# The input norm's vectors come as single rows and are spread by TensorE, the small loads go to SyncE's queue, and the first projection's copies stand in another order

## The chip, the cores and the metric

The kernel runs on one NeuronCore of a Trainium2 chip. The metric is the device time of one execution in microseconds (us); lower is better. A profile of one execution stands beside the timed runs, and each number in this part comes from it or from the times.

## What the kernel computes

A trunk of two layers over 512 tokens of width 1024, in float32. First comes a layer norm of the input with the vectors `ln_in_g` and `ln_in_b`. Each layer then projects the tokens to 2212 columns, runs three kinds of attention on them (latent, differential with a learned lambda, and forgetting), projects back and normalises, and sends the tokens through 16 experts of which each token uses two. Cut to what matters here:

```
h = layer_norm(x, ln_in_g, ln_in_b)
for l in range(DEPTH):
    mix = mixer_sublayer(h, ..., w_in[l], ...)      # starts with proj = h @ w_in
    h = layer_norm(ALPHA * h + mix, ln1_g[l], ln1_b[l])
    h = layer_norm(ALPHA * h + grouped_moe(h, router_w, router_bias, ...), ln2_g[l], ln2_b[l])
```

## The kernel before

The 512 tokens lie in four tiles `h[:, t]` of 128 partitions by 1024. Weights come in pieces of 128x1024 (512 KB), issued by `pump` (L324) on SyncE's queue. A piece is made into two rounded parts: `prep_hi` copies it on ScalarE (L369), `prep_lo` subtracts that copy from the piece on VectorE (L376). The tokens are split likewise in `make_hT`: TensorE transposes a tile into PSUM (L741), ScalarE copies the rounded part (L743), VectorE makes the rest (L744). A product is then three matmuls, `mm3`: L400 (high by high), L401 (low tokens by high weights), L402 (high tokens by low weights).

The beginning of the program, which this change touches:

- `setup` sends dummy matmuls (`busy`, L553, one column of weights by 384 columns) and issues the first loads in the order of the string `PRO`: x tile 0, the norm's two vectors, a table, two pieces of w_in, x tile 1, two pieces, x tiles 2 and 3. `load_ln` fetches each vector as a broadcast to 128 partitions, 512 KB.
- `ln` normalises one tile: the sum (ScalarE, L699), the mean (VectorE, L703), (x - mean) * g (VectorE, L721), the sum of squares (ScalarE, L706), the power -0.5 (GpSimd, L708), and times the rstd plus b (VectorE, L725).
- `token_major` with column group c0 is the first projection: for each tile the transposes, then 24 matmuls over the four pieces, then `ev_c0` (L823 to L830, a copy and a small rotary). Group c1 follows with its own four pieces, then the attention units, filled up with the other projections.
- `rotary8` and `consts` make small tables; `consts` also issues the small loads (router weights and bias, norm gains, lambda vectors) on ScalarE's queue and computes the lambdas.
- `score_consts` (at step 40 of the attention) makes `rg`, router weights times `ln1_g`, from the columns `lncol` (L1186, L1190).

The order of the instructions on each engine is set when the program is built, by a scheduler that works with estimated times; an engine takes its instructions in this order, and a wait holds all that stand behind it. Loads on SyncE's and ScalarE's queues share eight completion semaphores (named DMAHW0 to DMAHW7 in the program), so an issue also waits until the load that had its semaphore before has landed.

Of the kernel before, what the change touches and what calls it, by code (L numbers as in the profile page):

```python
# [11 lines left out]
F32 = mybir.dt.float32  # L12
# [4 lines left out]
AF = mybir.ActivationFunctionType  # L17
OP = mybir.AluOpType
# [5 lines left out]
S = 512  # L24
NT = 4
DEPTH = 2
NE = 16
# [28 lines left out]
WARM = 40  # L56
WARM2 = 6
# [203 lines left out]
class Kern:  # L261
# [238 lines left out]
    def setup(self):  # L500
# [30 lines left out]
        self.busy(WARM)  # L531
# [70 lines left out]
    def consts(self):  # L602
# [18 lines left out]
        nc.scalar.dma_start(self.rw, I["router_w"].rearrange("(h p k) e -> p h k e", h=2, k=4))  # L621
        self.rb = c.tile([128, NE], F32, name="rb")
        nc.scalar.dma_start(self.rb, self.bcast(I["router_bias"], NE))
        v.tensor_scalar(self.rb, self.rb, 0.5, None, op0=OP.add)
# [6 lines left out]
        with nc.allow_non_contiguous_dma(reason="small vectors"):  # L631
            for l in range(DEPTH):
                nc.scalar.dma_start(self.gq[:, l], I["mla_q_norm_g"][l].rearrange("(k p) -> p k", p=128))
                nc.scalar.dma_start(self.gkv[:, l], I["mla_kv_norm_g"][l].rearrange("(k p) -> p k", p=128))
                for s in range(2):
                    nc.scalar.dma_start(self.gs[64 * s:64 * s + 64, l:l + 1],
                                        I["diff_subln_g"][l].rearrange("(p o) -> p o", o=1))
                for j, n in enumerate(("diff_lam_q1", "diff_lam_k1", "diff_lam_q2", "diff_lam_k2")):
                    nc.scalar.dma_start(self.lamv[:, l, j], self.bcast(I[n][l], 32))
                nc.scalar.dma_start(self.fb[:, l:l + 1], I["fox_f_bias"][l].rearrange("(p o) -> p o", o=1))  # L640
# [15 lines left out]
        for x in hs + [self.hc]:  # L656
            x.free()

        self.nlam = c.tile([128, DEPTH], F32, name="nlam")
# [6 lines left out]
        hl.free()  # L666
# [25 lines left out]
    def ln_stats(self, z, sums=None, then=None, eps=LN_EPS):  # L692

        nc, v = self.nc, self.nc.vector
        st = self.sm.tile([128, 6], F32, name="bst", bufs=4)
        junk = self.lnbuf[2].f
        if sums is None:
            sums = [st[:, 0:1]]
            nc.scalar.activation(junk, z, AF.Copy, accum_out=sums[0])  # L699
        if len(sums) == 2:  # L700
            v.tensor_add(st[:, 0:1], sums[0], sums[1])
            sums = [st[:, 0:1]]
        v.tensor_scalar(st[:, 1:2], sums[0], -1.0 / D, None, op0=OP.mult)  # L703
        if then:
            then(st)
        nc.scalar.activation(junk, z, AF.Square, bias=st[:, 1:2], accum_out=st[:, 2:3])  # L706
        v.tensor_scalar(st[:, 3:4], st[:, 2:3], 1.0 / D, eps, op0=OP.mult, op1=OP.add)
        self.i_pow = nc.gpsimd.tensor_tensor(st[:, 4:5], st[:, 3:4], self.mhalf, OP.pow)  # L708
        return st

    def ln(self, z, sums=None, pool=False, eps=LN_EPS, out=None):
# [12 lines left out]
        if out is None:  # L724
            v.scalar_tensor_tensor(z, w, st[:, 4:5], self.lnrow[1], op0=OP.mult, op1=OP.add)  # L725
            return
# [29 lines left out]
    def token_major(self, l, c, evac, pre=None):  # L756
        ids = [self.idx[l, c, j] for j in range(4)]
        P = [self.get(i) for i in ids]
        if pre:
            pre(0)  # L760
            pre(1)
        for t in range(NT):
            if pre:
                if l and t == 0:
                    self.busy(WARM4)
                self.make_hT(t)
                if l == 0 and t == 0:
                    self.busy(WARM2)
# [47 lines left out]
    def w_in_phase(self, l, pre):  # L816
# [5 lines left out]
        def ev_c0(t, ps):  # L822
            nc.scalar.activation(tm[t], ps, AF.Copy)  # L823
# [6 lines left out]
            v.tensor_add(x[:, :, 0:8], a, b)  # L830
# [4 lines left out]
        if l == 0:  # L835
            self.consts()
# [10 lines left out]
        def turn(g, j):  # L847
# [9 lines left out]
            for a in range(2):  # L857
                x = [self.dm[g][a].r[32 * i:32 * i + 32, 512 * j:512 * j + 512] for i in range(3)]
                y = ps[32 * a:32 * a + 32]
                nc.scalar.activation(x[0], y, AF.Copy, scale=sc)  # L860
                nc.scalar.activation(x[1 if j else 2], y, AF.Copy, scale=sc)
                if j:
                    v.tensor_sub(x[2], y, x[0].bitcast(F32))
# [15 lines left out]
        self.token_major(l, "c1", ev_c1)  # L879
        self.cap = 2  # L880
# [253 lines left out]
    def mixer(self, l, pre):  # L1134
# [5 lines left out]
        nc.gpsimd.dma_start(gc, self.I["ln1_g"][l].rearrange("(h p k) -> p h k", h=2, k=4))  # L1140
        nc.gpsimd.dma_start(bc, self.I["ln1_b"][l].rearrange("(h p k) -> p h k", h=2, k=4))
# [40 lines left out]
        def score_consts():  # L1182
# [3 lines left out]
            nc.vector.tensor_tensor(self.rg, rw, gc.rearrange("p h (k o) -> p (h k) o", o=1).to_broadcast([128, 8, NE]), OP.mult)  # L1186
# [761 lines left out]
class Unit:  # L1948
# [6 lines left out]
    def scores(self):  # L1955
# [4 lines left out]
        for m in range(self.maps):  # L1960
# [17 lines left out]
            nc.vector.tensor_tensor_reduce(out=p[:, 0:n], in0=ps[:, 0:n], in1=b, op0=OP.add, op1=OP.min,  # L1978
# [97 lines left out]
```

## Time and profile before

| | us |
|---|---|
| median of 3 runs | 1391.88 (1390.42 to 1392.33) |
| profiled execution, its own time | 1390.85 |
| its span, first to last instruction | 1389.1 |
| TensorE busy | 1303.3 (94%) |
| first matmul of the c0 projection that runs without a break behind it (L401, tile 0) | 19.21 |
| first matmul of the c1 projection | 52.03 |

The profiled execution took 1.75 us more than its span and 1.03 us less than the median. A row of a timeline gives the start, the duration, the engine, the source line and the operation, and in brackets how long the engine had been idle and what ended that; several like instructions are merged (x8). In a table of windows each engine has its busy time in the stretch, then the granted TensorE clock (1.00 is 2.4 GHz, 0.50 is 1.2 GHz), the DMA engines' busy share and what they moved in GB/s.

### The profile page before, as it was taken

The numbers are of one execution on the slowest core, as the hardware profiler recorded it, in microseconds if no ns is written. First come the engines' busy times: TensorE is split into PE (matmuls) and PEld (weight loads), VectorE is DVE, ScalarE is ACT, GpSimd is POOL, SyncE is SP. The second block draws the span as 40 slices with busy tenths as digits, with TensorE's granted clock in tenths as the row PEclk, the third lists the DMA queues.
The fourth block names the chain that finished last, engine by engine and source line by source line (L and its number), as shares of the span: only waits on it lengthen the run. The fifth ranks groups of instructions, "written<-read, shape, count | busy, mean of one in ns | idle before, by whom it ended". The sixth has DMA issues, their size and how long they took to land. (4 is left out here: it accounts for less than half of the span.)

```text
span 1389.1 us, 18769 instructions
## 1 busy us (share of the span) xinstructions
PE 1303.3 (94%) x6052; PEld 961.6 (69%) x6052; DVE 1016.0 (73%) x2289; ACT 800.3 (58%) x1429; POOL 267.3 (19%) x208
## 2 busy tenths in 40 slices
PE   8999999989999999899799989999999999979994
PEld 5786766768677776677488766676877777656773
DVE  5768977676778777677655798867768877757775
ACT  5467856551566665566336776557146666555662
POOL 1012223332111211111000222224412111102110
PEclk9999999999999999999899999999999999989998
DMA  8411312257699997999510123325679999878991
GB/s 257 127 35 31 111 62 92 85 176 259 222 306 315 338 363 252 326 398 368 191 43 16 31 80 122 99 69 166 226 249 298 307 345 362 244 279 299 384 360 61
DMA packets 114426, 290.05 MB, mean 209 GB/s; under 512 B 19751, under 2 KB 42535, under 8 KB 114321
## 3 DMA queue, kind: packets, MB, share of 16 engines
q1 hardware_dynamic: 97824, 254.31, 52.1%
q0 software_dynamic: 11136, 31.38, 9.2%
q10 hardware_dynamic: 5360, 3.10, 0.8%
q8 instruction: 50, 0.82, 0.2%
q14 instruction: 56, 0.45, 0.1%
HBM read 268.13 MB, written 27.00 MB: 212 GB/s over the span
## 5 line engine op out<-in xcount | busy, mean ns | idle before, releaser
L369 ACT ACTIVATE slot<-arena 128x1024 fp32r<-128x1024 f32 (+3 forms) x147 | 127.4, 887 | 103.1 <-PE A L402 26.6
L376 DVE TENSOR_TENSOR slot<-slot,slot 128x1024 fp32r<-128x1024 f32 x105 | 128.3, 1225 | 64.7 <-ACT slot L369 61.9
L369 ACT ACTIVATE slot<-slot 128x1024 fp32r<-128x1024 f32 x111 | 117.1, 1058 | 100.4 <-PE A L402 36.7
L402 PE MATMUL S<-slot,rounded 128*128 128x512 f32 x368 | 150.4, 409 | 0.2 <-DVE slot L1844 0.2
L402 PE MATMUL A<-slot,rounded 128*128 128x512 f32 x372 | 147.7, 397 | 0.0
L400 PE MATMUL S<-slot,rounded 128*128 128x512 f32 x316 | 138.9, 442 | 6.4 <-ACT rounded L743 4.0
L376 DVE TENSOR_TENSOR slot<-arena,slot 128x1024 fp32r<-128x1024 f32 (+2 forms) x101 | 112.8, 1120 | 42.8 <-ACT slot L369 40.5
L401 PE MATMUL S<-slot,rounded 128*128 128x512 f32 x316 | 127.7, 404 | 3.0 <-DVE rounded L744 1.7
L400 PE MATMUL A<-slot,rounded 128*128 128x512 f32 x288 | 125.4, 435 | 0.3 <-ACT rounded L743 0.3
L1571 POOL DMA_INDIRECT yD<-arena,ix x28 | 46.9, 1674 | 408.1 <-ACT rounded L1606 197.5
L401 PE MATMUL A<-slot,rounded 128*128 128x512 f32 x288 | 114.1, 396 | 0.4 <-DVE rounded L744 0.4
L1989 ACT ACTIVATE arena<-arena,ast 128x256 f32<-128x256 f32 (+3 forms) x160 | 88.9, 557 | 33.1 <-DVE ast L1978 23.9
L378 POOL TENSOR_TENSOR slot<-arena,slot 128x1024 fp32r<-128x1024 f32 (+4 forms) x46 | 70.7, 1550 | 170.2 <-ACT slot L369 148.6
L369 ACT ACTIVATE rounded<-slot 128x1024 fp32r<-128x1024 f32 x70 | 74.3, 1061 | 44.6 <-PE A L401 25.5
L400 PE MATMUL S<-rounded,slot 128*128 128x512 f32 (+1 forms) x224 | 90.5, 406 | 0.0
L401 PE MATMUL S<-rounded,slot 128*128 128x512 f32 (+1 forms) x224 | 89.8, 401 | 0.0
L402 PE MATMUL S<-rounded,slot 128*128 128x512 f32 (+1 forms) x224 | 89.2, 398 | 0.0
L402 PEld LDWEIGHTS S<-slot,rounded 128*128 128x128 f32 x368 | 70.9, 193 | 17.7 <-DVE slot L1844 2.0
L402 PEld LDWEIGHTS A<-slot,rounded 128*128 128x128 f32 x372 | 70.1, 188 | 16.3
L2020 ACT ACTIVATE slot<-T 128x128 fp32r<-128x128 f32 (+3 forms) x128 | 53.4, 431 | 48.2 <-PE T L2015 47.5
L1647 PE MATMUL A<-slot,arena 128*128 128x512 f32 x168 | 79.4, 594 | 0.5 <-ACT arena L1605 0.5
L400 PEld LDWEIGHTS S<-slot,rounded 128*128 128x128 f32 x316 | 61.1, 194 | 25.4 <-ACT rounded L743 5.0
(368 smaller groups left out, 3066.8 us busy)
## 6 DMA issues: line engine op xcount, KB each, us to landing
slot<-in_exp_w_down_dram SPq DMA_DIRECT2D x80, 512.0 KB
slot<-in_exp_w_up_dram SPq DMA_DIRECT2D x73, 512.0 KB
slot<-in_exp_w_gate_dram SPq DMA_DIRECT2D x72, 512.0 KB
arena<-in_exp_w_gate_dram SPq DMA_DIRECT2D x60, 512.0 KB
arena<-in_exp_w_up_dram SPq DMA_DIRECT2D x59, 512.0 KB
arena<-in_exp_w_down_dram SPq DMA_DIRECT2D x52, 512.0 KB
arena<-in_w_in_dram SPq DMA_DIRECT2D x14, 512.0 KB
slot<-in_w_in_dram SPq DMA_DIRECT2D x12, 512.0 KB
```

The source lines that it names most:

```text
L369: self.nc.scalar.activation(hi, r, AF.Copy)
L376: self.nc.vector.tensor_sub(lo, r, hi.bitcast(F32))
L378: self.nc.gpsimd.tensor_tensor(lo, r, hi.bitcast(F32), OP.subtract)
L400: t.matmul(ps, xh, wh, start=start, stop=False)
L401: t.matmul(ps, xl, wh, start=False, stop=False)
L402: t.matmul(ps, xh, wl, start=False, stop=stop)
L1571: self.nc.gpsimd.indirect_dma_start(out=self.yD[:, :], out_offset=bass.IndirectOffsetOnAxis(ap=ix[:, 0:1], axis=0), in_=y, in_offset=None, ...
L1647: nc.tensor.matmul(ps, xW(e)[:, kk], P.raw.f[:, 512 * k:512 * k + 512], start=kk == 0, stop=kk == 7)
L1989: nc.scalar.activation(p, p, AF.Exp, bias=self.st[:, m:m + 1], scale=-1.0, accum_out=self.st[:, 2 + m:3 + m])
L2020: nc.scalar.activation(self.part(0), self.ps, AF.Copy)
```

## The change

The two norm vectors come as one row each (4 KB) on ScalarE's queue; TensorE multiplies a 1x128 row of ones with each half row, which puts it on 128 partitions of PSUM, and VectorE (g) and ScalarE (b) copy it to SBUF. The dummy matmuls go from 40 to 8 and 14. The small loads are merged over layers and issued from SyncE's queue; the lambdas are computed after the c1 projection. `token_major` prepares the first pieces in an order written out by hand, and `issue_after` holds groups of instructions behind named ones of the same engine.

```
-WARM = 40
+WARM = (8, 14)
...
-                self.load_ln(I["ln_in_g"], I["ln_in_b"], nc.sync)
+                self.spread_ln(I["ln_in_g"], I["ln_in_b"])
...
+    def spread_ln(self, g, b):
+        nc = self.nc
+        self.lnbuf = [self.unit(self.A) for _ in range(5)]
+        self.iw = 1
+        self.lnrow = [x.f for x in self.lnbuf[0:2]]
+        one = self.cp.tile([1, 1], F32, name="one")
+        nc.vector.memset(one, 1.0)
+        rows = [x.f[0:1] for x in self.lnbuf[3:5]]
+        for row, x in zip(rows, (g, b)):
+            nc.scalar.dma_start(row, x.rearrange("(o d) -> o d", o=1))
+        self.busy(WARM[0])
+        self.lps = [self.psS.tile([128, 512], F32, name="S") for _ in range(4)]
+        for j, ps in enumerate(self.lps):
+            nc.tensor.matmul(ps, one.to_broadcast([1, 128]), rows[j // 2][:, 512 * (j % 2):512 * (j % 2) + 512], start=True, stop=True)
+        self.busy(WARM[1])
+        nc.vector.tensor_copy(self.lnrow[0][:, 0:512], self.lps[0])
...
-        nc.scalar.dma_start(self.rw, I["router_w"].rearrange("(h p k) e -> p h k e", h=2, k=4))
+        nc.sync.dma_start(self.rw, I["router_w"].rearrange("(h p k) e -> p h k e", h=2, k=4))
...
-            for l in range(DEPTH):
-                nc.scalar.dma_start(self.gq[:, l], I["mla_q_norm_g"][l].rearrange("(k p) -> p k", p=128))
...
+            nc.sync.dma_start(self.gq, I["mla_q_norm_g"].rearrange("l (k p) -> p l k", p=128))
...
+        lps = getattr(self, "lps", None)
+        if lps:
+            v.tensor_copy(self.lnrow[0][:, 512:1024], lps[1])
...
+        if lps:
+            with self.tc.issue_after(i.ins):
+                for n in range(2):
+                    self.i_b = nc.scalar.activation(self.lnrow[1][:, 512 * n:512 * n + 512], lps[2 + n], AF.Copy)
...
+        if pre and l == 0:
+            self.prep_limit = 1
+            self.prep()
+            self.prep_limit = 2
             pre(0)
-            pre(1)
+            with self.tc.issue_after(self.i_b.ins):
+                with self.tc.issue_after(self.i_ln.ins):
+                    self.prep_low(1)
+                    self.make_hT(0)
+                    self.busy(WARM2)
+                    P = [self.get(i) for i in ids[:2]]
+                    self.prep_limit = len(self.pieces)
+                    pre(1)
+                    P += [self.get(i) for i in ids[2:]]
...
-        nc.gpsimd.dma_start(gc, self.I["ln1_g"][l].rearrange("(h p k) -> p h k", h=2, k=4))
+        nc.sync.dma_start(gc, self.I["ln1_g"][l].rearrange("(h p k) -> p h k", h=2, k=4))
...
-            nc.vector.tensor_tensor(self.rg, rw, gc.rearrange("p h (k o) -> p (h k) o", o=1).to_broadcast([128, 8, NE]), OP.mult)
+            with self.tc.issue_after(self.i_red.ins):
+                nc.vector.tensor_tensor(self.rg, rw, gc.rearrange("p h (k o) -> p (h k) o", o=1).to_broadcast([128, 8, NE]), OP.mult)
```

VectorE at the start of the program, before (`bst` holds a tile's norm statistics, `arena` is the shared SBUF region that holds x times g and the weight pieces, `slot` a piece's rounded part, `T` and `S` are PSUM):

```order
L588 CAST arena<-arena 128x4
L1186 TENSOR_TENSOR rg<-rw,lncol_698 128x128
L703 TENSOR_SCALAR bst<-bst 128x1
L624 TENSOR_SCALAR rb<-rb 128x16
L721 SCALAR_TENSOR_TENSOR arena<-h,bst,arena 128x1024
L707 TENSOR_SCALAR bst<-bst 128x1
L725 SCALAR_TENSOR_TENSOR h<-arena,bst 128x1024
L376 TENSOR_TENSOR slot_162<-arena,slot_161 128x1024
L672 TENSOR_SCALAR gs<-gs 128x1
L376 TENSOR_TENSOR slot_165<-arena,slot_164 128x1024
L744 TENSOR_TENSOR rounded<-T,rounded 128x512
```

The same place after (the lines are those of the changed file: L723 is L703 of before, L749 L721, L753 L725, L772 L744, L605 L588):

```order
L585 COPY arena<-S 128x512
L726 COPY arena<-S 128x512
L723 TENSOR_SCALAR bst<-bst 128x1
L749 SCALAR_TENSOR_TENSOR arena<-h,bst,arena 128x1024
L735 TENSOR_SCALAR bst<-bst 128x1
L753 SCALAR_TENSOR_TENSOR h<-arena,bst 128x1024
L376 TENSOR_TENSOR slot_150<-arena,slot_149 128x1024
L376 TENSOR_TENSOR slot_194<-arena,slot_193 128x1024
L772 TENSOR_TENSOR rounded<-T,rounded 128x512 x2
L723 TENSOR_SCALAR bst<-bst 128x1
L605 CAST arena<-arena 128x4
L376 TENSOR_TENSOR slot_227<-arena,slot_226 128x1024
```

Ahead of tile 0's mean there now stand the two copies of g, and no longer `rg`, `rb`, `gs` or the cast of the positions.

ScalarE at the same place, before, with the loads that it issues:

```order
L699 ACTIVATE arena,bst<-h 128x1024
L634 DMA gkv<-in_mla_kv_norm_g_dram 128x2x1
L706 ACTIVATE arena,bst<-h,bst 128x1024
L636 DMA gs<-in_diff_subln_g_dram 64x1 x2
L639 DMA arena<-in_diff_lam_k_dram 128x32
L640 DMA fb<-in_fox_f_bias_dram 4x1
L633 DMA gq<-in_mla_q_norm_g_dram 128x3x1
L369 ACTIVATE slot_161<-arena 128x1024
L634 DMA gkv<-in_mla_kv_norm_g_dram 128x2x1
L636 DMA gs<-in_diff_subln_g_dram 64x1
L369 ACTIVATE slot_164<-arena 128x1024
L743 ACTIVATE rounded<-T 128x512
```

And after (L719 is L699 of before, L729 L706, L771 L743, L604 the issue of the positions):

```order
L719 ACTIVATE arena,bst<-h 128x1024
L369 ACTIVATE slot_149<-arena 128x1024
L729 ACTIVATE arena,bst<-h,bst 128x1024
L733 ACTIVATE arena<-S 128x512 x2
L369 ACTIVATE slot_193<-arena 128x1024
L719 ACTIVATE arena,bst<-h 128x1024
L604 DMA arena<-in_positions_dram 128x4x1
L771 ACTIVATE rounded<-T 128x512 x2
```

The eight small loads between tile 0's sum and the copy of its transposes are gone from ScalarE; the load of the positions moved from the program's start to here, and the copies of b came in.

VectorE ahead of tile 1's low part (the second L772 of tile 1 follows later):

```order
L700 TENSOR_SCALAR arena<-arena 128x16
L723 TENSOR_SCALAR bst<-bst 128x1
L701 TENSOR_SCALAR arena<-arena 128x16
L749 SCALAR_TENSOR_TENSOR arena<-h,bst,arena 128x1024
L702 SCALAR_TENSOR_TENSOR arena<-arena 128x16
L703 SCALAR_TENSOR_TENSOR arena<-arena 128x16
L735 TENSOR_SCALAR bst<-bst 128x1
L704 SCALAR_TENSOR_TENSOR arena<-arena 128x16
L753 SCALAR_TENSOR_TENSOR h<-arena,bst 128x1024
L705 TENSOR_SCALAR arena<-arena 128x16
L772 TENSOR_TENSOR rounded<-T,rounded 128x512
```

The whole norm of x tile 2 (L749, L753) stands ahead of the low part of tile 1 (L772); before, only its first half stood there.

## Rows read from the trace of the kernel before

**Rows 1.** The page, busy time of each engine, share of the span, instructions

```profile
PE 1303.3 (94%) x6052; PEld 961.6 (69%) x6052; DVE 1016.0 (73%) x2289; ACT 800.3 (58%) x1429; POOL 267.3 (19%) x208
```

**Rows 2.** The timeline of the first 20 us, tile 0's chain

```profile
4.84 1.06 ACT L699 ACTIVATE arena<-h 128x1024 f32<-128x1024 f32 x1 [2.12 <-DMA h<-in_x_dram]
...
5.54 0.17 DVE L588 CAST arena<-arena 128x4 f32<-128x4 int32 x1 [3.98 <-DMA arena<-in_positions_dram]
...
9.14 0.29 DVE L1186 TENSOR_TENSOR rg<-rw,lncol 128x128 f32<-128x128 f32 x1 [3.43 <-DMA rw<-in_router_w_dram]
...
9.54 1.15 ACT L706 ACTIVATE arena<-h,bst 128x1024 f32<-128x1024 f32 x1 [3.54 <-DVE bst L703]
...
11.05 0.57 POOL L708 TENSOR_TENSOR bst<-bst,mhalf 128x1 f32<-128x1 f32 x1 [8.12 <-DVE bst L707]
...
11.65 1.28 DVE L725 SCALAR_TENSOR_TENSOR h<-arena,bst 128x1024 f32<-128x1024 f32 x1 [0.69 <-POOL bst L708]
...
12.99 1.16 PE L741 MATMUL T<-cst,h 128*128 128x128 f32 x8 [1.32 <-DVE h L725]
...
16.24 1.06 ACT L369 ACTIVATE slot<-arena 128x1024 fp32r<-128x1024 f32 x1 [2.63 <-DMA gs<-in_diff_subln_g_dram]
...
17.21 0.58 ACT L743 ACTIVATE rounded<-T 128x512 fp32r<-128x512 f32 x1
...
19.21 0.79 PE L401 MATMUL S<-slot,rounded 128*128 128x512 f32 x1 [0.58 <-DVE bst L703]
```

**Rows 3.** Windows: stretch, length, busy of the engines, clock, DMA share, GB/s

```profile
5.00:6.00 1.00, 1.00 (x5) 0.42 (x4) 0.17 (x1) 0.99 (x2) 0.00 (x0) 1.00 1.01 377
...
14.00:15.00 1.00, 0.41 (x3) 0.08 (x1) 0.87 (x1) 0.00 (x0) 0.00 (x0) 1.00 0.55 70
17.00:18.00 1.00, 0.16 (x1) 0.17 (x1) 0.67 (x1) 1.00 (x3) 0.00 (x0) 0.66 1.07 406
24.00:25.00 1.00, 1.00 (x5) 0.79 (x4) 0.83 (x1) 0.25 (x2) 0.00 (x0) 0.92 0.21 61
38.00:40.00 2.00, 2.00 (x7) 1.54 (x6) 0.40 (x4) 0.00 (x0) 0.00 (x0) 0.50 1.11 277
```

**Rows 4.** The timeline of TensorE, tiles 1 to 3 and the c1 projection

```profile
28.02 0.47 PE L401 MATMUL A<-slot,rounded 128*128 128x512 f32 x1
...
37.48 0.53 PE L401 MATMUL S<-slot,rounded 128*128 128x512 f32 x1 [1.75 <-DVE rounded L744]
...
44.50 1.05 PE L741 MATMUL T<-cst,h 128*128 128x128 f32 x8
...
52.03 0.40 PE L400 MATMUL S<-slot,rounded 128*128 128x512 f32 x1
```

**Rows 5.** Waits of SyncE's queue to 60 us: total, times, longest

```profile
SPq L324 <- DMA gs<-in_diff_subln_g_dram: 5.0, 2, 4.0
```

**Rows 6.** The timeline, prices: dummy matmuls, VectorE's spacing, plain float32 matmuls

```profile
6.83 0.13 PEld L553 LDWEIGHTS <-b_zero 128*1 128x1 bf16 x1 [0.19 <-issue]
7.13 4.15 PEld L553 LDWEIGHTS <-b_zero 128*1 128x1 bf16 x26 [0.17 <-issue]
...
19.25 1.28 DVE L721 SCALAR_TENSOR_TENSOR arena<-h,bst,arena 128x1024 f32<-128x1024 f32 x1
...
20.46 1.22 DVE L376 TENSOR_TENSOR slot<-arena,slot 128x1024 fp32r<-128x1024 f32 x1
...
350.29 1.88 PE L1647 MATMUL A<-arena 128*128 128x512 f32 x4
```

**Rows 7.** Groups by line and form, VectorE: busy, mean ns, idle before

```profile
L918 DVE COPY arena<-S 128x512 f32<-128x512 f32 x7 | 4.8, 692 | 9.3 <-PE S L402 9.3
```

**Rows 8.** The timeline, later: SyncE's queue and the use of lncol

```profile
87.98 0.56 SPq L324 DMA_DIRECT2D slot<-in_w_in_dram  x1
...
238.65 0.95 PE L1190 MATMUL S<-rw,lncol 128*1 128x16 f32 x32
...
250.44 0.34 SPq L324 DMA_DIRECT2D arena<-in_exp_w_gate_dram  x1
```

More of the change, by code (lines that the diff above doesn't have):

```diff
@@ L631, in consts @@
         with nc.allow_non_contiguous_dma(reason="small vectors"):
-            for l in range(DEPTH):
-                nc.scalar.dma_start(self.gq[:, l], I["mla_q_norm_g"][l].rearrange("(k p) -> p k", p=128))
[L634 to L640, printed above, removed]
+            nc.sync.dma_start(self.gq, I["mla_q_norm_g"].rearrange("l (k p) -> p l k", p=128))
+            nc.sync.dma_start(self.gkv, I["mla_kv_norm_g"].rearrange("l (k p) -> p l k", p=128))
+            for s in range(2):
+                nc.sync.dma_start(self.gs[64 * s:64 * s + 64], I["diff_subln_g"].rearrange("l p -> p l"))
+            for j, n in enumerate(("diff_lam_q1", "diff_lam_k1", "diff_lam_q2", "diff_lam_k2")):
+                x = I[n]
+                nc.sync.dma_start(self.lamv[:, :, j], bass.AP(tensor=x.tensor, offset=x.offset, ap=[[0, 128], [32, DEPTH], [1, 32]]))
+            nc.sync.dma_start(self.fb, I["fox_f_bias"].rearrange("l p -> p l"))
         hs = [self.half() for _ in range(6)]
@@ L657, in consts, with lambdas @@
             x.free()
+        self.hl = hl
+    def lambdas(self):
+        nc, c, v = self.nc, self.cp, self.nc.vector
         self.nlam = c.tile([128, DEPTH], F32, name="nlam")
@@ L665, in consts @@
                                        op0=OP.mult, op1=OP.mult, accum_out=d[:, l, j:j + 1])
-        hl.free()
+        self.hl.free()
+        v.tensor_scalar(self.rb, self.rb, 0.5, None, op0=OP.add)
         nc.scalar.activation(d, d, AF.Exp)
@@ L757, in token_major @@
         ids = [self.idx[l, c, j] for j in range(4)]
-        P = [self.get(i) for i in ids]
-        if pre:
+        if pre and l == 0:
+            self.prep_limit = 1
+            self.prep()
+            self.prep_limit = 2
             pre(0)
-            pre(1)
+            with self.tc.issue_after(self.i_b.ins):
[7 more added lines that the diff above has]
+                    P += [self.get(i) for i in ids[2:]]
+        else:
+            P = [self.get(i) for i in ids]
+            if pre:
+                pre(0)
+                pre(1)
         for t in range(NT):
@@ L765, in token_major @@
                     self.busy(WARM4)
-                self.make_hT(t)
-                if l == 0 and t == 0:
-                    self.busy(WARM2)
+                if l or t:
+                    self.make_hT(t)
                 if l in PRL:
@@ L822, in ev_c0 @@
         def ev_c0(t, ps):
-            nc.scalar.activation(tm[t], ps, AF.Copy)
+            i = nc.scalar.activation(tm[t], ps, AF.Copy)
+            if t == 0:
+                self.i_tm = i
             x = tm[t].rearrange("p (m d) -> p m d", m=16)
@@ L829, in ev_c0 @@
                                 self.s8[:, t, j:j + 1].to_broadcast([128, 16, 4]), OP.mult)
-            v.tensor_add(x[:, :, 0:8], a, b)
+            i = v.tensor_add(x[:, :, 0:8], a, b)
+            if t == 0:
+                self.i_rot = i
         self.token_major(l, "c0", ev_c0, pre)
@@ L835, in w_in_phase @@
         if l == 0:
-            self.consts()
+            with self.tc.issue_after(self.i_tm.ins):
+                with self.tc.issue_after(self.i_rot.ins):
+                    self.consts()
         else:
@@ L879, in w_in_phase @@
         self.token_major(l, "c1", ev_c1)
+        if l == 0:
+            with self.tc.issue_after(self.i_turn.ins):
+                with self.tc.issue_after(self.i_turnv.ins):
+                    self.lambdas()
         self.cap = 2
@@ L1977, in scores @@
             K.ip[m] += 1
-            nc.vector.tensor_tensor_reduce(out=p[:, 0:n], in0=ps[:, 0:n], in1=b, op0=OP.add, op1=OP.min,
+            K.i_red = nc.vector.tensor_tensor_reduce(out=p[:, 0:n], in0=ps[:, 0:n], in1=b, op0=OP.add, op1=OP.min,
                                            scale=1.0, scalar=3e38, accum_out=self.st[:, m:m + 1])
```

15 lines of the change are left out of this document (7 added, 8 removed).

## The prediction

> **What bounds the kernel now.** I read the page first: TensorE is busy for 94% of the span [rows 1], so over most of the program only its own work counts, and a change is worth what it takes out of TensorE's idle or slow time. The edits lie almost all in the first 52 us, so I then read the timeline of that stretch and followed what TensorE waits for.
>
> Tile 0 [rows 2]: x lands at 4.84 and ScalarE sums it within some 1.2 us. The mean should follow at 6, but VectorE's next instruction is L1186, the router's product, and it waits until 9.14 for a router load; the sum of squares therefore starts at 9.54 and the normalised tile at 11.65 (ready at 12.93). The transposes are done by 14.15. ScalarE should now copy them, but it stands in the row of small loads that it has to issue; its next piece copy (L369) starts only at 16.24, 2.63 us idle behind a load of `gs`, and the copy of the transposes at 17.21. VectorE, behind its own piece, gives the low part so that L401 runs at 19.21. From there on TensorE has enough.
>
> The windows show two more things [rows 3]. First, the granted clock: TensorE did little from 14.4 to 17.8, and the clock falls from 2.4 to 1.2 GHz at about 17.6 and is back at about 24. A second hole ends at 37.48 [rows 4], and the stretch of 38 to 40 is at 1.2 GHz again. Second, the DMA engines, which moved 377 GB/s between 5 and 6 us, move 70 between 14 and 15: SyncE's queue, which carries x and w_in, was waiting for a small load of ScalarE's queue, 5.0 us in two waits [rows 5].
>
> Tile 2's L401 comes at 37.48, tile 3's transposes at 44.50 (7.02 later, part of it at the low clock), and the c1 projection starts at 52.03, 7.53 behind those transposes [rows 4]. From 46 us on I see no hole of 1 us in TensorE's timeline until the attention. So I measure the change by one number: when does c1 start?
>
> **The change, step by step.**
>
> *x and the weights.* Two vectors of 512 KB leave the queue ahead of the first piece, and the small loads leave the semaphores that x and w_in need. At 350 GB/s (a little under the 377 of [rows 3]) x, the table and four pieces of 0.52 MB with x tile 1 between them follow each other by 1.5 us: the first piece at about 6, x tile 1 at 9, x tile 2 at 13, x tile 3 at 14.5. None is the last that something waits for below, with at least 1 us to spare.
>
> *Spreading the vectors.* No row shows these four products; the nearest are the plain float32 products of L1647. Each shows as two records, so four records in 1.88 us [rows 6] are 0.86 us a product at full clock, 1.72 at half. The dummies are 0.32 us apart up to 7.1 us (0.13 and 0.19 idle) and 0.16 after it (26 in 4.15) [rows 6]: the low clock lasts until then. So: dummies from 1.44 to 4.0, two products of g to about 7.5, six dummies and two products of b at full clock to 10.0. The two copies of g cost VectorE 0.69 each [rows 7]; the second ends at 8.2 and stands ahead of the mean. That is the new head of the chain: x's sum, ready at 6, waits for the spread vector. Were the clock high from 4 us on, this would be 1.6 us earlier; were the rows 1.5 us later than dummy number eight, at most that much later.
>
> *Tile 0.* Mean at 8.2, squares at 8.3; from squares to normalised start took 2.11 before (9.54 to 11.65 [rows 2]), so 10.4; but ScalarE copies b behind the squares, two at 0.55, to 10.75. Start 10.8, end 12.05, against 12.93: 0.9 earlier. VectorE then subtracts two pieces (1.22 each, the successor some 0.08 before its end [rows 6], so 2.3) and makes tile 0's low part (0.7): L401 at about 15.0 against 19.21, 4.2 earlier. ScalarE is ready for it: behind the copies of b stand one piece (1.06) and one sum (1.2), so the high part starts at 12.8. TensorE's idle time before it is about 1 us, so I take the clock as high here.
>
> *Tile 1.* From 15.0 on VectorE is the bound: second low part 0.6, piece 1.15, first half of x tile 1's norm 1.2, piece 1.15, second half 1.28, with small ones 20.5. TensorE ends tile 0 at 20.4. Then comes the order that I count against the change: the whole norm of x tile 2 stands ahead of tile 1's low part. Its squares wait for tile 0's copy on ScalarE (21.1 to 22.3), the power (0.57 [rows 2]) gives 23.2, its second half ends at 24.4, and the low part at 25.1. L401 of tile 1 at 25.2 against 28.02 [rows 4]: 2.8 earlier, and a hole of some 4 us with one matmul in it.
>
> *The clock.* Before, holes of 3.4 and about 2 us were each followed by the low clock [rows 3, 4]. I therefore take it as low in the first part of tile 1: 23 matmuls at 0.233 are 5.4 us, and the low stretch adds about 1.6 (7.02 in tile 2 of before, against 5.4). It is back near the end of the tile, as at 24 to 25 us in [rows 3]. Tile 1 ends at 32.2.
>
> *Tiles 2 and 3.* From the end of a tile to the next L401 it is 2.3 us where VectorE is held by x tile 3's norm and the rotary of tile 1: 34.5 against 37.48. No new hole of over 2 us, so full clock: tile 2 ends at 39.8. From there 7.5 us as before (44.50 to 52.03): **c1 at 47.3 against 52.03, 4.7 earlier**.
>
> *Small loads on SyncE's queue.* Thirteen issues of 0.3 to 0.6 us stand behind the last piece of w_in and ahead of an expert piece, the zeroing store and the piece issued at 87.98 [rows 8]. Even at 5 us each over eight semaphores they land by 50, so they cost nothing; without that cover (some 40 us) the w_in piece would be late. The lambdas move to the first attention steps, where fillers of 24 matmuls each (5.6 us) keep TensorE busy. For layer 1 the two columns `lncol` stand in SyncE's queue ahead of four expert pieces and wait for layer 0's use of the same buffer (238.65); the first piece behind them was issued at 250.44 anyway [rows 8], so 11 us of cover. The Trainium skill (DMA: Bandwidth & Descriptors, Issuing engines are not separate DMA queues) holds that the issuing queue saves only the time to issue; the 5.0 us in [rows 5] differ, since here queues share semaphores. By the rule the move to SyncE would be worth nothing, and the sum here takes nothing for it beyond the freed waits.
>
> *The rest* (two table loads of ScalarE fewer, two issues of GpSimd, `rg` in the attention): off TensorE's path, 0 to 0.3 us. I take 0.
>
> After the projection the order on all engines is nearly that of before, loads start when buffers come free, and so an earlier c1 moves all that follows. Against the profiled 1390.85 the sum is 1386.15; the median of the runs lies 1.03 higher, at 1391.88, so I forecast **1387.2**.
>
> **The rivals.** A timed difference under 0.2% (2.8 us) is about what a measurement of this kernel can't tell from none.
>
> 1. *The clock falls twice.* Tile 2 waits 2.3 us for its low part; if that hole is enough, another 1.7 go: c1 at 49.0, 3.0 earlier, 1388.9. For it: the hole before 37.48 was no longer. Against: transposes lie in it. Chance 0.20.
> 2. *The positions hold VectorE.* Their load, 512 elements of 4 bytes, landed 4.8 us after its issue before (0.73 to 5.54 [rows 2]). It is now issued at about 10, beside a full queue, and L605 stands ahead of the third piece at 15.5. Each us beyond 15.5 moves the chain by as much; at 18, c1 is at 49.7, 1389.6. Chance 0.12.
> 3. *The clock stays high.* Tile 1 ends at 30.5 and c1 starts at 46.0: 6.0 earlier, 1385.9. For it: tile 0's last matmuls and the transposes lie in the hole's first part. Chance 0.17.
> 4. *Given back later.* The earlier start meets a transfer bound to nothing before; 1391.9, no change. Nothing in the rows speaks for it. Chance 0.04.
> 5. *Slower.* SyncE's queue is held by the `lncol` wait of layer 1 beyond 250.44, which it does if `score_consts` runs over 11 us later than before or those loads wait for a semaphore of a store; four expert pieces come late and TensorE waits some 8 us, less the 4.7: 1395. Chance 0.05.
>
> **How the numbers follow.** The forecast has 0.42. The range must hold the forecast with about 1 us on either side for the transfers and the spread (0.42), rival 1 (0.20), rival 3 (0.17) and the nearer half of rival 2: 1384.8 to 1390.0. "Faster" is below 1389.1: the forecast, rival 3, just over half of rival 1 and a third of rival 2, 0.42 + 0.17 + 0.11 + 0.04 = 0.74; of that I move 0.03 to the others, as all my tile times hang on one order of VectorE. Within 0.2%: 0.22. Slower: 0.07.
>
> **What would show it.** In the changed kernel's timeline: two products of a row by ones up to about 7.5, VectorE's copies of g right behind, the mean at 8.2; tile 0 normalised by 12 and its L401 at 15.0; no wait of SyncE's queue for a small load; L401 of tile 1 at 25.2 behind x tile 2's norm; the clock low once, in tile 1; c1 at 47.3. I am wrong if VectorE is not the bound between 15 and 25 us, if the clock behaves otherwise (1.7 us for each stretch), or if c1 is early and the span is not.

## The result and the profile after

The changed kernel takes 1384.86 us (median of 7 runs, 1383.48 to 1388.73), the kernel before 1391.88 (median of 7, 1389.59 to 1394.45): ratio 0.995, 95% interval 0.9934 to 0.9966, so 4.7 to 9.2 us faster. The forecast said 1387.2 and 1384.8 to 1390.0. The time lies just inside the low end of that range, but, as the runs below show, for another reason than the forecast's.

The page after, span and busy time of the engines [rows 1]:

```profile
span 1381.7 us, 18726 instructions
...
PE 1295.2 (94%) x6034; PEld 959.4 (69%) x6042; DVE 1017.1 (74%) x2292; ACT 799.4 (58%) x1429; POOL 265.0 (19%) x204
```

The span is 7.4 us shorter, and TensorE's own busy time 8.1 us. Had the first stage lost its holes, idle time would have gone, not busy time. That is the first sign that the gain lies elsewhere.

The timeline of TensorE in the changed kernel, from the first dummy to c1 [rows 2, 4]:

```profile
1.43 2.72 PE L552 MATMUL A<-mchunk,b_zero 128*1 128x384 bf16 x8 [1.43 <-DVE one L576]
4.08 3.77 PE L583 MATMUL S<-arena,one 1*128 1x512 f32 x4
7.79 2.08 PE L552 MATMUL A<-mchunk,b_zero 128*1 128x384 bf16 x6
9.79 3.78 PE L583 MATMUL S<-arena,one 1*128 1x512 f32 x4
13.50 3.84 PE L552 MATMUL A<-mchunk,b_zero 128*1 128x384 bf16 x12
17.28 1.16 PE L769 MATMUL T<-cst,h 128*128 128x128 f32 x8
...
19.41 0.50 PE L401 MATMUL S<-slot,rounded 128*128 128x512 f32 x1
...
30.05 0.50 PE L401 MATMUL A<-slot,rounded 128*128 128x512 f32 x1 [2.07 <-DVE rounded L772]
...
37.02 1.04 PE L769 MATMUL T<-cst,h 128*128 128x128 f32 x8
...
46.52 0.50 PE L401 MATMUL A<-slot,rounded 128*128 128x512 f32 x1 [0.22 <-DVE rounded L772]
...
51.88 0.39 PE L400 MATMUL S<-slot,rounded 128*128 128x512 f32 x1
```

c1 starts at 51.88, against 52.03 before: 0.15 us earlier, not 4.7. The second pair of products still takes 3.78 us, as long as the first, and the twelve dummies behind it are 0.32 us apart: TensorE runs at 1.2 GHz until the trace records its first rise at 17.06 us (the clock column shows 1.00 until a first change is recorded, so before it one reads the spacing). VectorE and ScalarE in the same stretch:

```profile
6.19 0.69 DVE L585 COPY arena<-S 128x512 f32<-128x512 f32 x1 [4.72 <-PE S L583]
7.89 0.69 DVE L726 COPY arena<-S 128x512 f32<-128x512 f32 x1 [1.01 <-PE S L583]
8.50 0.14 DVE L723 TENSOR_SCALAR bst<-bst 128x1 f32<-128x1 f32 x1
...
14.31 1.29 DVE L753 SCALAR_TENSOR_TENSOR h<-arena,bst 128x1024 f32<-128x1024 f32 x1 [4.20 <-ACT arena L733]
```

```profile
8.68 1.15 ACT L729 ACTIVATE arena<-h,bst 128x1024 f32<-128x1024 f32 x1 [1.25 <-DVE bst L723]
...
11.90 0.60 ACT L733 ACTIVATE arena<-S 128x512 f32<-128x512 f32 x1 [1.98 <-PE S L583]
13.61 0.60 ACT L733 ACTIVATE arena<-S 128x512 f32<-128x512 f32 x1 [1.11 <-PE S L583]
```

VectorE stands 4.20 us at L753, with all of tile 0 ready but the vector b; before, L725 started at 11.65 [rows 2]. Windows of TensorE for the clock [rows 3] and all engines for the transfers:

```profile
27.90:30.00 2.10, 0.08 (x1) 1.00 1.16 287
31.00:34.00 3.00, 3.00 (x9) 0.50 0.04 9
35.00:37.00 2.00, 2.00 (x10) 1.00 0.87 245
```

```profile
14.00:15.00 1.00, 1.00 (x4) 0.38 (x3) 0.69 (x1) 1.00 (x2) 0.00 (x0) 1.00 1.09 362
```

One fall of the clock, in tile 1, behind the hole before 30.05; and 362 GB/s where it was 70.

SyncE's queue waited for small loads to 60 us (total, times, longest):

```profile
SPq L324 <- DMA arena<-in_positions_dram: 5.2, 1, 5.2
...
SPq L936 <- DMA arena<-in_diff_lam_q_dram: 2.5, 1, 2.5
...
SPq L936 <- DMA arena<-in_diff_lam_k_dram: 0.8, 1, 0.8
```

Of the 7.4 us, then, 7.3 lie behind c1's start (span less c1: 1337.1 before, 1329.8 after). They are not at one place: over long stretches the same product comes some 0.1 us earlier every 15 us (from 350 to 500 us, 1.1 us). Between such stretches stand steps of 1 to 4 us either way, and the falls of the clock come at other places in the two traces; at 600 us the changed kernel was 0.1 us behind, at 700 us 3.9 ahead. Behind c1 the clock was low for 63.0 us of the one trace and 59.4 of the other, so up to 1.8 us of this pair's difference (half of 3.6) can be the clock's: the size has to come from timed runs. I took the starts of successive 512-column products from the trace (clock high, gaps over 300 ns left out, only products whose 512 columns lie side by side in memory). Between 45 and 350 us one follows the other by 231.8 ns in the mean before, and by 228.8 after. The simplest place to see it is tile 3 of c0: from its first L401 to c1's start there are 23 intervals without a wait, 5.47 us before (46.56, the row here, to 52.03 [rows 4]) and 5.36 after (46.52 to 51.88).

```profile
46.56 0.50 PE L401 MATMUL A<-slot,rounded 128*128 128x512 f32 x1 [0.22 <-DVE rounded L744]
```

### The profile page after: what moved, and what is told of

Read it like the earlier page. It is cut to its first block, busy times and chain, and to the rows that moved or that the text cites. A ratio compares the mean times of both kernels' runs of the same rounds, so it can differ in the third digit from the quotient of the medians.

```text
span 1381.7 us, 18726 instructions
## 1 busy us (share of the span) xinstructions
PE 1295.2 (94%) x6034; PEld 959.4 (69%) x6042; DVE 1017.1 (74%) x2292; ACT 799.4 (58%) x1429; POOL 265.0 (19%) x204
## 5 line engine op out<-in xcount | busy, mean ns | idle before, releaser
L369 ACT ACTIVATE slot<-slot 128x1024 fp32r<-128x1024 f32 x111 | 117.2, 1059 | 95.5 <-PE A L402 35.9
L402 PE MATMUL S<-slot,rounded 128*128 128x512 f32 x368 | 148.5, 404 | 0.3 <-DVE slot L376 0.2
L400 PE MATMUL S<-slot,rounded 128*128 128x512 f32 x316 | 137.0, 436 | 3.7 <-ACT rounded L771 1.3
L401 PE MATMUL S<-slot,rounded 128*128 128x512 f32 x316 | 125.8, 398 | 1.0 <-DVE rounded L1926 0.7
L401 PE MATMUL A<-slot,rounded 128*128 128x512 f32 x288 | 114.0, 396 | 2.3 <-DVE rounded L772 2.3
L400 PE MATMUL S<-rounded,slot 128*128 128x512 f32 (+1 forms) x224 | 89.3, 400 | 0.0
L401 PE MATMUL S<-rounded,slot 128*128 128x512 f32 (+1 forms) x224 | 88.4, 395 | 0.0
L402 PE MATMUL S<-rounded,slot 128*128 128x512 f32 (+1 forms) x224 | 88.1, 393 | 0.0
```

Of the source, the lines that this page charges most:

```text
L369: self.nc.scalar.activation(hi, r, AF.Copy)
L400: t.matmul(ps, xh, wh, start=start, stop=False)
L401: t.matmul(ps, xl, wh, start=False, stop=False)
L402: t.matmul(ps, xh, wl, start=False, stop=stop)
```

## The experiments

Two questions: where do the 7 us come from, and why did the first stage give nothing? All kernels were timed against the kernel before in five rounds. "Tile 3" is that stretch of 23 intervals, from each run's own timeline; c1 is its start in the profiled execution. That start is uncertain by some us: in the four runs whose instructions are those of before (both executions of it, and those with padding behind and ahead) it lies between 48.42 and 52.03.

| run | c1 us | tile 3 us | ratio to before, 95% |
|---|---|---|---|
| before, again | 49.50 | 5.47 | 1.0009 (0.9988 to 1.0029) |
| changed, again | 53.48 | 5.35 | 0.9948 (0.9930 to 0.9966) |
| spread only | 55.03 | 5.35 | 0.9969 (0.9952 to 0.9986) |
| changed without spread | 43.04 | 5.46 | 0.9961 (0.9945 to 0.9976) |
| before, 32 bytes of padding | 51.73 | 5.37 | 0.9944 (0.9924 to 0.9964) |
| changed, 32 bytes more | 49.18 | 5.46 | 1.0005 (0.9986 to 1.0025) |
| changed without spread, padded | 42.87 | 5.34 | 0.9903 (0.9881 to 0.9925) |
| without spread, one-row dummies | 50.42 | 5.47 | 1.0023 (1.0004 to 1.0043) |
| loads only | 46.77 | 5.47 | 0.9960 (0.9942 to 0.9978) |
| order only | 49.90 | 5.46 | 0.9979 (0.9960 to 0.9999) |
| changed, products of 128 rows | 48.54 | 5.35 | 0.9919 (0.9892 to 0.9945) |
| before, padding ahead | 48.42 | 5.47 | 1.0017 (1.0001 to 1.0034) |

**Program or execution?** Both kernels again, unchanged, and the change split at the spread.

> The kernel before, unchanged. In its first profile a 512-column product follows the last by 231.8 ns in the mean between 45 and 350 us; in the changed kernel by 228.8, and some 2,500 such products make about 7 us, the whole gain, while c1 starts only 0.15 us earlier. If that interval comes with the program (theory of the stream), this copy shows 231 to 233 ns again and its time is 0 from the kernel before. If it comes with the execution or the chip (theory of the execution), this copy shows 228 to 229 like the changed kernel beside it. Either way the ratio is 1.000, and its interval says what a difference has to exceed.

> The changed kernel, unchanged, on the same chip as the copy of the kernel before. Both theories: 0.995 again, c1 at 51.9. Theory of the stream: interval of the 512-column products 228 to 229 ns where the copy of before has 231 to 233. Theory of the execution: the same interval in both, and then the 5 to 7 us must be found at places that the two traces do not share (falls of the clock, waits).

Spread only is the kernel before with `spread_ln` and with the copies of g and b in `ln_stats` as changed:

```diff
-WARM = 40
+WARM = (8, 14)
...
-        self.busy(WARM)
...
-                self.load_ln(I["ln_in_g"], I["ln_in_b"], nc.sync)
+                self.spread_ln(I["ln_in_g"], I["ln_in_b"])
```

> The kernel before with the spread of the norm's vectors and its dummies (8 and 14) alone; the loads, their queues and the order of the copies as before. Forecast's mechanism, corrected by the trace after (the clock stays at 1.2 GHz through the products, b's copies end at 14.2): x and w_in land 1.5 us earlier, but the mean still stands behind the router's product on VectorE and the copies of b end later than the norm of before did (11.65), so c1 starts 0 to 2 us later than 52.03, ratio 1.000 to 1.0015. Theory of the stream: another 0.995 is possible, if the spread's instructions are what shifts the interval to 228; the interval in its trace says so.

Without spread, the changed kernel has these lines the other way round, and nothing waits for the copies of b, as there are none:

```diff
-WARM = (8, 14)
+WARM = 40
...
+        self.busy(WARM)
...
-                self.spread_ln(I["ln_in_g"], I["ln_in_b"])
+                self.load_ln(I["ln_in_g"], I["ln_in_b"], nc.sync)
...
-            with self.tc.issue_after(self.i_b.ins):
+            if True:
```

> The changed kernel with the two vectors loaded in full on SyncE's queue as before and 40 dummies at the head as before; all else as changed. If the spread cost its 2.7 us at tile 0 (second half of the norm at 14.31 against 11.65) and the rest gave what the forecast gave it, L401 of tile 0 comes at 15 to 16 and c1 at 47.5 to 49: 3 to 4 us faster than the changed kernel, ratio to before 0.992 to 0.993. If the first stage is bound by VectorE's order and not by the spread, c1 is at 51 to 52, ratio 0.995. Theory of the stream: the interval decides on top, 3 ns of it being 7 us.

The short interval comes with the spread: 228.8 and 228.9 ns in the two kernels that have it, 231.3 and 231.2 in the two that have not. It is the program's, not the execution's. Spread only delays c1, by 3 us or more and so more than I had written, and is yet 0.9969. And without the spread c1 starts at 43.04, some 9 us earlier than in the changed kernel and 4.5 us earlier than I expected; the trace has no fall of the clock between its first rise, at 5.82 us, and 142 us:

```profile
1.43 8.80 PE L553 MATMUL A<-mchunk,b_zero 128*1 128x384 bf16 x40 [1.43 <-DVE ones L596]
10.17 1.16 PE L770 MATMUL T<-cst,h 128*128 128x128 f32 x8
...
12.66 0.48 PE L401 MATMUL S<-slot,rounded 128*128 128x512 f32 x1
```

(TensorE's timeline of the kernel without the spread.) Its time is nevertheless no better than the changed kernel's.

**An address?** The spread allocates a tile of one number, `one`, in the pool of constants. It takes 32 bytes a partition, and what is allocated behind it moves by 32: in the compiled programs the 22 buffers of the pool of slots begin at 138080 + 4096 n before (32 modulo 64) and at 138112 + 4096 n after (0 modulo 64). `arena` (34432) and `rounded` (91776) are allocated earlier and stay at 0. Each of the next three kernels is one named in the table with one more line:

```diff
+        self.pad = c.tile([128, 8], F32, name="pad")
         self.bzero = c.tile([128, 128], BF, name="b_zero")
```

> The kernel before with one unused tile of 32 bytes a partition in the pool of constants; not an instruction differs. The row of ones that the spread needs takes 32 bytes in that pool, and the pool of slots (the high and low parts that TensorE reads) lies behind it: its buffers begin at 32 modulo 64 in the kernel before (138080) and at 0 modulo 64 in the changed kernel (138112). Theory of the address: the interval of the 512-column products between 45 and 350 us falls from 231.5 to 228.8 ns, c1 still starts at 49 to 52, ratio 0.995. Theory of the instructions (the interval comes with the order or number of TensorE's instructions): 231.5 ns and 1.000.

> The changed kernel with another unused tile of 32 bytes, so that the slots begin at 32 modulo 64 again (138144). Theory of the address: interval 231.5 ns, ratio to before 0.999 to 1.001, and the change as it was meant is worth nothing. Theory of the instructions: 228.8 ns and 0.995 as without the tile.

> The changed kernel with the vectors loaded in full and 40 dummies as before, and the unused tile of 32 bytes: the early c1 (43.0) and the aligned slots together. Theory of the address: c1 at 43, interval 228.8 ns, ratio 0.9961 - 0.0055 = 0.9905, below both kernels. Theory of the instructions: 0.996, as without the tile.

All three came as the theory of the address has it. TensorE's timeline of tile 3 in the kernel before, unchanged, and in the kernel before with the unused tile:

```profile
44.03 0.50 PE L401 MATMUL A<-slot,rounded 128*128 128x512 f32 x1 [0.23 <-DVE rounded L744]
...
49.50 0.40 PE L400 MATMUL S<-slot,rounded 128*128 128x512 f32 x1
```

```profile
46.36 0.50 PE L401 MATMUL A<-slot,rounded 128*128 128x512 f32 x1 [0.22 <-DVE rounded L745]
...
51.73 0.39 PE L400 MATMUL S<-slot,rounded 128*128 128x512 f32 x1
```

Not one instruction differs, and 23 intervals take 5.37 us instead of 5.47. By operands (the moving one, which is streamed, against the stationary one, the weights in the array), before and padded: slots against `rounded` 233.4 and 229.8 ns (1,700 products), both operands in `rounded` 230.7 and 229.5 (610), `rounded` against slots 235.4 and 234.0 (170). That makes 6.1 + 0.7 + 0.2 = 7.0 us. The count leaves out the products that read `rounded` in four stretches of 128 columns against slots: 234.1 and 228.7 (398 with 128 weight columns), 2.1 us more, so 9.1. The padded kernel measured 0.9944, 7.8 us (5.0 to 10.6 by its interval). The changed kernel with 32 bytes more is at 1.0005: **as the change was meant, it is worth nothing that can be measured**. The third pair agrees: without the spread 0.9961 unpadded and 0.9903 padded.

**Which buffers?** The kernel before with the same unused tile ahead of `arena` and `rounded`:

```diff
+        self.pad = c.tile([128, 8], F32, name="pad")
         self.A = Arena(c.tile([128, NA], F32, name="arena"), NA, False)
```

> The kernel before with the unused tile of 32 bytes ahead of the pools arena and rounded instead of behind them: the slots begin at 0 modulo 64 as in the run with the tile behind (0.9944), but arena and rounded, at 0 in every kernel so far, now begin at 32. By operand the interval of the 512-column products was, before and with the tile behind: slots as the moving operand 233.4 and 229.8 ns (1,700 products), rounded as the moving operand with rounded weights 230.7 and 229.5 (610). Theory of the moving operand (only the buffer that streams 512 columns counts, whatever its pool): slots 229.8, rounded 3 to 4 ns up to 233 to 234.5, so some 780 products lose about 3 us of the 7: ratio 0.9960 to 0.9970. Rival (something of the pool of slots, not the 64 bytes): rounded stays at 229.5 to 230.7, ratio 0.9944. Second rival (both operands count alike): slots above 231, ratio 0.998 to 1.000.

```profile
42.95 0.50 PE L401 MATMUL A<-slot,rounded 128*128 128x512 f32 x1 [0.23 <-DVE rounded L745]
...
48.42 0.40 PE L400 MATMUL S<-slot,rounded 128*128 128x512 f32 x1
```

The first two theories failed: the slots begin at 0 modulo 64 and still show 233.4 ns, and the ratio is 1.0017 (1.0001 to 1.0034). The third had the slots right and the ratio nearly (0.998 to 1.000), but if each operand counted by its own address, products with both in `rounded`, now at 32, should have become slower, and they show 230.6 as before. So it is not the slots' address alone. Short intervals appear only where slots, `arena` and `rounded` all begin at 0 modulo 64, and long ones where either side is at 32.

**The clock.** Why did it stay low in the changed kernel with TensorE busy all the time? The rows of a matmul are the partitions that it reads: 128 in the dummies, one in the spread's products.

One-row dummies in the changed kernel without spread:

```diff
-            self.nc.tensor.matmul(ps[0:1, 0:384], self.bzero[:, 0:1], self.mask["mchunk"][:, 0:384], start=True, stop=True)
+            self.nc.tensor.matmul(ps[0:1, 0:384], self.bzero[0:1, 0:1], self.mask["mchunk"][0:1, 0:384], start=True, stop=True)
```

> The changed kernel with the vectors loaded in full, and each of the dummies with one row instead of 128: the same columns and the same spacing, no slot moved. In the run with 128 rows the clock was at 2.4 GHz from 7 us on and stayed there through tile 3. With the spread it rose only at 17.1, although TensorE was never idle from 1.4 us on, and what stood between the dummies were products of one row. Theory of the rows (products of one row don't bring the clock up): it stays at 1.2 GHz until tile 0's own products, L401 of tile 0 near 13, some 5 to 6 us into them, tile 0 ends 4 us later and c1 starts at 45 to 48. Rival (only the kind of product, plain float32, or its duration matters): up at 7, c1 at 43. The whole: 2 to 4 us over the run without that edit, ratio 0.998 to 0.999, by the first; 0.996 by the second.

```profile
1.43 12.96 PE L553 MATMUL A<-mchunk,b_zero 1*1 1x384 bf16 x40 [1.43 <-DVE ones L596]
14.32 1.97 PE L770 MATMUL T<-cst,h 128*128 128x128 f32 x8
16.22 2.07 PE L553 MATMUL A<-mchunk,b_zero 1*1 1x384 bf16 x6
18.22 0.79 PE L400 MATMUL S<-slot,rounded 128*128 128x512 f32 x1
```

Forty dummies of one row take 12.96 us, 0.32 each from the first to the last, where forty of 128 rows took 8.80. The clock's first rise is at 22.47 us, 4.2 us into tile 0's own products. The theory of the rows holds; I had written 2 to 4 us, and it is 7.4 us at c1 and 8.6 us in the time (1.0023 against 0.9961), as the clock also falls once more, at 36 us. The counterpart, products of 128 rows in the changed kernel's `spread_ln`:

```diff
-WARM = (8, 14)
+WARM = (10, 14)
...
-        one = self.cp.tile([1, 1], F32, name="one")
-        nc.vector.memset(one, 1.0)
-        rows = [x.f[0:1] for x in self.lnbuf[3:5]]
+        one = self.cp.tile([128, 128], F32, name="one")
+        self.pad = self.cp.tile([128, 8], F32, name="pad")
+        nc.vector.memset(one, 0.0)
+        nc.vector.memset(one[0:1], 1.0)
+        rows = [x.f for x in self.lnbuf[3:5]]
+        nc.vector.memset(rows[0], 0.0)
+        nc.gpsimd.memset(rows[1], 0.0)
...
-            nc.scalar.dma_start(row, x.rearrange("(o d) -> o d", o=1))
+            nc.scalar.dma_start(row[0:1], x.rearrange("(o d) -> o d", o=1))
```

The stationary side is then `one` itself.

> The changed kernel with products of 128 rows for the spread: the vectors lie in row 0 of buffers that are zeroed first, and the stationary side has ones in row 0 alone; the same columns. Two dummies more ahead (10), as the rows come some 0.7 us later, and the pool padded so that the slots begin at 0 modulo 64 like the changed kernel's. Theory of the rows: the clock is up at 4 to 7.1 us and stays there through the spread, the four products take 0.9 each at the high clock, the copies of b end at 10 to 11, the second half of tile 0's norm starts at 10.5 to 11.5 (14.31 with one row), c1 at 44 to 47 instead of 51.9 to 53.5, ratio 0.990 to 0.992. Rival (plain float32 products keep the clock low whatever their rows): up at 17 again, c1 at 52 to 54, ratio 0.995.

```profile
1.43 5.59 PE L552 MATMUL A<-mchunk,b_zero 128*1 128x384 bf16 x25 [1.43 <-DVE b_zero L530]
7.38 3.67 PE L587 MATMUL S<-arena,one 128*128 128x512 f32 x8 [0.35 <-DMA arena<-in_ln_in_g_dram]
10.98 0.97 PE L552 MATMUL A<-mchunk,b_zero 128*1 128x384 bf16 x5
13.11 1.16 PE L773 MATMUL T<-cst,h 128*128 128x128 f32 x8 [1.16 <-DVE h L757]
```

The four products take 3.67 us, where two took 3.78 with one row, and the trace has the clock at 2.4 GHz from 4.24 to 28.13 us. Here 25 dummies stand ahead of the products, not eight, so the rise is theirs; what the products show is that the clock stayed up through them. The row g came only at 7.4 (its load was issued behind b's and a table load), so c1 is at 48.54, 1.5 us beyond what I expected but 3.3 to 4.9 earlier than with one row, and the ratio is 0.9919. The misaligned changed kernel shows the same from the other side: there the clock happened to be up at 4.05, the two products of g took 1.98 us, and it fell at 7.46 although TensorE did not rest. Its windows:

```profile
4.10:7.40 3.30, 3.30 (x12) 1.35 (x12) 1.96 (x4) 2.54 (x4) 0.00 (x0) 1.00 0.97 340
7.50:14.00 6.50, 6.50 (x16) 2.01 (x14) 3.61 (x5) 3.87 (x7) 0.55 (x1) 0.50 1.03 404
```

**Loads or order?** Each alone, vectors loaded in full. Loads only is the changed kernel without spread, with `token_major` of before and:

```diff
-            with self.tc.issue_after(self.i_tm.ins):
-                with self.tc.issue_after(self.i_rot.ins):
-                    self.consts()
+            self.consts()
```

Order only is the kernel before with the changed `token_major`:

```diff
+        if pre and l == 0:
+            self.prep_limit = 1
...
             pre(0)
-            pre(1)
...
+                with self.tc.issue_after(self.i_ln.ins):
+                    self.prep_low(1)
+                    self.make_hT(0)
...
```

> The kernel before with the loads alone: small loads merged on SyncE's queue, the lambdas and the router's product behind other work, lncol on SyncE's queue; vectors loaded in full, copies in the order of before, slots at 32 modulo 64. Both parts together (the run without the spread) start c1 at 43.0 against 49.5 to 52.0. Theory of the loads (the small loads held the mean of x tile 0, the copies of ScalarE and SyncE's queue, and the clock fell in the holes): the mean at 6, tile 0's L401 at 13 to 14, no fall of the clock before tile 3, c1 at 43 to 45, ratio 0.996 to 0.998. Rival (the order is what counts): c1 at 48 to 50, ratio 0.999.

> The kernel before with the order of the copies in the first projection alone (first piece, tile 0's transposes and low part, then the rest); loads, their queues and the router's product where they were, vectors loaded in full, slots at 32 modulo 64. Theory of the loads: the router's product on VectorE still holds the mean until a router load lands (9.1 us before), tile 0's L401 comes at 15 to 18, c1 at 48 to 51, ratio 0.999 to 1.000. Rival (order): c1 at 44 to 46, ratio 0.997.

The loads bring the early start: mean of x tile 0 at 5.85 us, L401 at 12.92, and c1 at 46.77, later than expected by 1.8 us as the clock falls once, at 30. The order alone leaves VectorE behind `rg` until 7.83 and c1 at 49.90; its ratio, 0.9979, is lower than the 0.999 I gave, with an interval that reaches 0.9999. In a single profiled execution that c1 can't be told from those of the kernel before. VectorE with the loads only:

```profile
5.85 0.15 DVE L724 TENSOR_SCALAR bst<-bst 128x1 f32<-128x1 f32 x1 [0.36 <-ACT arena L720]
6.70 1.28 DVE L750 SCALAR_TENSOR_TENSOR arena<-h,bst,arena 128x1024 f32<-128x1024 f32 x1 [0.70 <-DMA arena<-in_ln_in_g_dram]
...
8.71 1.28 DVE L754 SCALAR_TENSOR_TENSOR h<-arena,bst 128x1024 f32<-128x1024 f32 x1 [0.67 <-POOL bst L737]
```

Both together start c1 another 3.7 us earlier (43.04), but the ratio stays (0.9961 against 0.9960, each uncertain by 0.0017).

## Why the prediction was right, and where it was wrong

The total came out in the range by luck, because two errors cancel: 4.7 us were forecast in the first stage and did not come, and about 7 us came from an address that no term of the sum contained.

**Right.** The transfers: no gap in the DMA engines from 2 to 17 us. The price of a spread product: its two records start 0.85 us apart at the low clock and 0.43 at the high one, 1.7 and 0.86 a product (forecast 1.72 and 0.86). The spread of g: the two products end at 7.8 (forecast 7.5), the second copy at 8.6 (8.2), the mean comes at 8.50 (8.2). Tile 1's hole: VectorE works on x tile 2's norm (L753 at 28.03) ahead of tile 1's low part (29.31), as counted. One fall of the clock, in tile 1. The small loads and `lncol` on SyncE's queue cost nothing: the layer-1 columns were issued at 238.79 us and the next expert piece at 249.96, with nothing late [rows 8].

**Wrong: "no wait of SyncE's queue for a small load".** It waited 5.2 us for the positions, whose load ScalarE issued at 13.73, behind the copies of b and not at about 10. The next piece was issued at 18.66, and the DMA engines moved nothing between 18 and 19 us. The zeroing store, L936, waited 2.5 and 0.8 us for lambda vectors. No wait of TensorE from 15 to 80 us names a load, and VectorE took the positions at 19.93 without a wait, so rival 2 did not come.

**Wrong: "six dummies and two products of b at full clock to 10.0".** I took the rise at 7.1 us from a kernel in which 40 dummies of 128 rows stood without a break. Here TensorE was as busy, but with products of one row in between. The clock rose at 17.06, b's products ended at 13.5 instead of 10.0, and the dummies, twice as long each, stood ahead of the transposes until 17.28. Tile 0's L401 came at 19.41 instead of 15.0, tile 1's at 30.05 instead of 25.2, c1 at 51.88 instead of 47.3. None of my rivals had this: the first and third asked whether the clock falls or stays, not whether the spread lets it rise. That the rows are the cause is shown from both sides, by the one-row dummies, which left the clock low, and the 128-row products, which did not bring it down.

So the loads and the order were worth more than I thought, 6.5 to 9 us at c1 (43.04 against 49.50 and 52.03), and the spread took it back (51.88, 53.48 and, with 32 bytes more, 49.18). Aligned kernels measure the spread's cost in the whole: 0.9948 with it, 0.9903 without, 6.3 us; the others 1.0005 and 0.9961, 6.1 us. Each ratio is uncertain by some 0.002, 2.5 us.

**Missing: the 32 bytes.** I read the diff for instructions and waits. A new constant of four bytes was not on the list.

**Still open.** First, how the address acts. With VectorE, ScalarE and GpSimd all idle, slot products still follow each other by 233.0 ns before (211 cases) and 228.4 padded (191), so it is not contention with those engines; nor is it with transfers, as slots against `rounded` show 233.6 (406 cases) and 228.9 (398) with no packet on any DMA engine. Whether moving and stationary operand must be at 0, or only agree, is not told apart: all three at 32 was not tried. Two readings of the traces speak for the second. Both operands in `rounded` show 230.6 ns at 0 and at 32 alike (before, and padding ahead); and products of 256 columns with both operands in slots and 128 weight columns show 117.2 ns at 32 and 116.9 at 0 (before and padded, 64 and 66 cases). And products with both operands in `rounded`, at 0 in both kernels, gained 1.2 ns, which neither rule explains. Second, c1's start is not the whole: without the spread, unpadded, c1 is 6.5 to 9 us early and the time 5.4 us (3.3 to 7.7) better. The traces show falls of the clock at other places later on; I did not isolate them. Rival 4, "given back later", was thus not as empty as its 0.04.

**A version that beats both**: the loads and the order of the change, the vectors loaded in full, 40 dummies, and the 32 bytes: 0.9903, median 1377.67 us against 1392.17 before in the same rounds.

## What to carry to other kernels

When a small change speeds up everything behind it by the same fraction, compare the interval between equal instructions first, then the addresses of what they read; a tile nobody reads is the control. And judge a dummy that is to keep TensorE's clock up by its rows as well as its time: here one-row matmuls filled TensorE without raising the clock. A forecast that meets its range is not yet explained: here every time given for TensorE in the first stage behind 9 us was wrong.

## What the runs showed of the hardware

- 32 bytes of displacement between slots and `rounded` cost 3.6 ns of 230 for each 512-column float32r product that streams a slot (233.4 against 229.8 ns in 1,700 products), 7.8 us of 1392 in the whole (5.0 to 10.6). Plain float32 products of a slot against `arena` did not change (436.0 and 436.5 ns from one record to the next, 177 and 178 cases). The Trainium skill (SBUF — State Buffer, Specifications (TRN2)) gives lines of 16 bytes and a penalty for crossing into a new line; by that a shift by 32 bytes, two whole lines, should change nothing. The measurement differs, and it decides.
- TensorE busy without a break, at 1.2 GHz: 13 us of one-row dummies left the clock low, and in one run it fell from 2.4 to 1.2 GHz while one-row products filled TensorE (3.30 us busy of 3.30 before the fall, 6.50 of 6.50 behind it). The same columns in products of 128 rows kept it at 2.4 GHz.
- Products of 512 float32r columns, each with new weights, stand 229.8 ns apart at the high clock even when aligned. The Trainium skill (TensorE: Matmul & The Clock Gate, Wait — 56ns, not 53.3ns?) gives 215.7 for 512 columns at that clock; the few bf16 products of `cum` against `b_zero` in these traces show it, 216.0.
- The start of c1 of one and the same program moved by 1.6 to 2.5 us between two executions (52.03 and 49.50; 51.88 and 53.48), with the first rise of the clock at 7.09 and 4.18, 17.06 and 19.00 us.
